# Splitting a norm's multiplications between GpSimd and VectorE: every other chunk instead of all of them

## The chip, the cores and the metric

The kernel runs on one core of one Trainium2 chip. Five engines work side by side, each on its own list of instructions in order: TensorE (PE in the rows; its weight loads are a row of their own, PEld), VectorE (DVE), ScalarE (ACT), GpSimd (POOL) and SyncE (SP, which here only issues DMAs). The metric is the device time of one execution in microseconds (us), the median of the runs.

## The reference, cut to what matters

Two transformer blocks follow each other on 256 tokens of width 1024 in float32. The second block has two layers; a layer is a SwiGLU feed-forward, a mixer (a convolution with latent attention in layer 0, sparse attention in layer 1) and a second feed-forward. In front of each of these stands a normalization with a modulation:

```python
def rms_norm_2(x, g):
    xf = x.astype(jnp.float32)
    y = xf * lax.rsqrt(jnp.mean(xf * xf, axis=-1, keepdims=True) + EPS)
    return (y * g.astype(jnp.float32)).astype(x.dtype)

def modulate(x, g, shift, scale):
    return rms_norm_2(x, g) * (1 + scale[:, None]) + shift[:, None]
...
        h = modulate(x, norm_g[l, 0], sh1, sc1)
        x = x + 0.5 * g1[:, None] * swiglu(h, ff_w13[l, 0], ff_w2[l, 0])
        h = modulate(x, norm_g[l, 1], sh2, sc2)
        ...
        x = x + g2[:, None] * y
        h = modulate(x, norm_g[l, 2], sh3, sc3)
        x = x + 0.5 * g3[:, None] * swiglu(h, ff_w13[l, 1], ff_w2[l, 1])
```

So per channel there is one gain (norm_g times 1 + scale) and one shift, and per token one factor, the reciprocal root of the mean square.

## The kernel before, in words

**Layout.** The residual stream `x` lies transposed in SBUF: the 1024 channels are 8 chunks of 128 partitions, the 256 tokens lie along the free dimension. The norm's output `h` is kept the same way, and split: a high part `hi` (rounded to the matmul's float32r) and a low part `lo`, the remainder. Each weight tile is split likewise into `whi` (ACT copies, line 359) and `wlo` (DVE subtracts, line 466), and a product is three matmuls or, in wide form, one of 512 columns and one of 256. Of weights, `pump` (line 453) splits three steps of 8 tiles ahead; the DVE half of a split is emitted one split later than the ACT half, so it never waits for it.

**The norm in two phases.** While the stage before ends, `norm_part` (line 627) takes each finished chunk c of x: `hi` and `lo` of x times gain go into `h` without the token factor (ACT at line 359, DVE at line 634), ACT squares the chunk, POOL adds the squares up (line 656). For the chunks in `st["keep"]` POOL also computes `xg` = x times gain into a buffer (line 640). The next stage's matmuls start on that `h` at once: the first two pairs of output tiles, the head, are computed without the token factor, and it is multiplied in when they are evacuated (`un`, line 532). Meanwhile `norm_sum` and `norm_bc` find the token factor and spread it over all partitions (`rbs`).

**`norm_apply`** (line 710) then makes the full `h` for the pairs that follow. For each chunk: the product `nt` = x times gain times `rbs`, either by POOL from `xg` and `rbs` (line 717) or, where no `xg` is there, by DVE in one fused instruction from x, the gain and `rbs` (line 719); then ACT writes `hi` = `nt` + shift (line 359), and DVE writes `lo` = `nt` + shift - `hi` (line 724, line 726 for the last chunk of a call). `lo` is emitted one chunk late.

**Order.** The program is one list of steps emitted in order, and each engine runs its own instructions in that order. `normed` (line 733) lays the steps out for a head of two pairs: three weight steps of the head, `norm_apply` on chunks 0 to 3, the head's fourth weight step (its emission puts one `whi` on ACT and one `wlo` on DVE), `norm_apply` on chunks 4 to 7, then `behind`: another split, and the evacuation of the head's second pair (line 531 and 532 on DVE, then ACT). Then come the pairs that read the full `h`, chunk by chunk from 0 to 7. Accumulators for them take turns in two PSUM buffers per tag; the fourth pair of a stage takes those that the second pair's evacuation frees.

**Five such norms** have a head of two pairs: in front of the mixer of layer 0 (near 620 us in the profile), the feed-forwards near 718, 910 and 1235 us, and the mixer of layer 1 (near 1102 us). The feed-forward near 428 us has a head of three pairs, and makes its `xg` in a step of its own (line 755); the norm at the end of the program keeps three chunks. In the feed-forwards a pair's evacuation also puts a fused step (line 1536) and a split of its result (line 392) on DVE.

Of the kernel before, what the change touches and what calls it, by code (L numbers as in the profile page):

```python
# [27 lines left out]
KD = D // P  # L28
# [275 lines left out]
class Kernel:  # L304
# [428 lines left out]
    def normed(self, st, gs, width=D, eps=1e-6, gain=None, shift=None, head=0, table=None, after=()):  # L733

        quiet = lambda xs: [setattr(x, "quiet", True) for x in xs]
        n1 = Step(lambda: self.norm_sum(st, width, eps, table=table))
        n2 = Step(lambda: self.norm_bc(st))
        if not head:
            quiet(gs[:2])
            return gs[:1] + [n1] + gs[1:2] + [n2] + gs[2:]  # L740

        def behind():
            self.pump(self.at, SPLIT_AHEAD + 1)
            st["behind"]()
            self.second()
        ap = [Step(lambda c=c: self.norm_apply(st, gain, lambda c: shift()[:, c:c + 1], c, c + 4)) for c in (0, 4)]
        e = 2 * head
        at = 2 if head == 2 else 3
        st["shift"] = shift
        if "two" not in st and head == 2:  # L750
            st["keep"] = range(KD)
        def times_gain():
            for c in range(KD):
                st["xg", c] = self.g("xg")
                self.nc.gpsimd.tensor_scalar(st["xg", c], self.x[:, c, :], gain(c), None, op0=OP.mult)
        out = gs[:1] + [n1] + ([Step(times_gain)] if head == 3 else []) + gs[1:at] + [n2] + gs[at:e - 1]
        out += [ap[0]] + gs[e - 1:e] + [ap[1], Step(behind)] + list(after) + gs[e:]
        quiet(gs[:e + 2])
        return out
# [1224 lines left out]
```

## Time and profile before

| | us |
|---|---|
| median of the runs shown | 1428.98 |
| lowest and highest of three runs | 1428.35, 1430.75 |
| the profiled execution, its own time | 1430.66 |
| its span, first to last instruction | 1428.9 |
| PE, DVE, ACT, POOL busy | 1400.3, 1139.2, 833.5, 213.4 |

The profile is one execution. "Busy" of PE says that a matmul was in flight; since matmuls are pipelined, a short wait can be hidden in it, and the weight loads (PEld) show it better. A row's "idle before" is the time in which an engine stood still ahead of the instruction, with the instruction that ended that. In a timeline, neighbouring instructions of one kind are merged: "x3" and the time from the start of the first to the end of the third.

### The profile page before, as it was taken

What the parts mean: (1) busy time and instruction counts of PE and PEld (TensorE: products, weight loads), DVE (VectorE), ACT (ScalarE), POOL (GpSimd) and SP (SyncE); (2) the same over time, 40 slices, a digit from 0 to 9 for tenths busy, and PEclk for the clock granted to TensorE, in tenths of its full rate; (3) what the DMA queues carried; (4) which work ended last, traced back from release to release, by engine and by line L of the source; (5) the groups of instructions that cost most, each with busy time, mean ns of one, the idle gap of its engine ahead of it and who ended that gap; (6) DMA issues with size and microseconds to landing.
All of it is one profiled execution on the core that took longest, in us unless ns stands there. A gap on an engine that the chain in (4) does not pass through costs nothing.

```text
span 1428.9 us, 23142 instructions
## 1 busy us (share of the span) xinstructions
PE 1400.3 (98%) x8998; PEld 1231.8 (86%) x8998; DVE 1139.2 (80%) x1911; ACT 833.5 (58%) x1605; POOL 213.4 (15%) x199
## 2 busy tenths in 40 slices
PE   8999999999999999999999999999999999999997
PEld 8887999888898888899888888888888877988886
DVE  7877877998879887878788888898887786887653
ACT  6646556765456665466675645665645565665542
POOL 3000101000142001421420003200033100500021
PEclk9999999999999999999999999999999999999999
DMA  9344534778775768744367778586776510376540
GB/s 330 123 148 147 207 129 167 270 268 319 296 290 193 293 263 307 267 160 150 117 236 265 270 284 305 202 314 254 277 289 227 207 60 31 148 266 235 199 181 34
DMA packets 46046, 311.66 MB, mean 218 GB/s; under 512 B 5232, under 2 KB 7024, under 8 KB 9072
## 3 DMA queue, kind: packets, MB, share of 16 engines
q1 hardware_dynamic: 45936, 310.19, 58.6%
q8 instruction: 70, 1.15, 0.3%
q14 instruction: 40, 0.33, 0.1%
HBM read 309.12 MB, written 1.05 MB: 217 GB/s over the span
## 4 chain that ended last, share of the span: by engine, by line
PE 83%; DVE 10%; ACT 3%; DMA 2%; issue 1%; POOL 0%; SPq 0%; POOLq 0%; ACTq 0%; DVEq 0%
PE mm L395 75%; DVE wlo L466 3%; PE o L395 2%; PE sc L395 2%; PE mmt L395 1%; DVE h L724 1%; DMA raw<-w_in 1%; PE ada L395 1%; DVE p L980 1%; PE pT L987 1%; PE ssum L395 1%; ACT p L359 1%; ACT whi L359 1%; DMA raw<-w 1%; DVE nm L969 1%
## 5 line engine op out<-in xcount | busy, mean ns | idle before, releaser
L395 PE MATMUL mm<-h,whi 128*128 128x512 f32 (+2 forms) x2400 | 708.3, 357 | 5.8 <-DVE h L724 3.8
L395 PE MATMUL mm<-h,wlo 128*128 128x256 f32 (+1 forms) x1960 | 553.1, 282 | 2.0 <-DVE wlo L466 2.0
L466 DVE TENSOR_TENSOR wlo<-raw,whi 128x1024 fp32r<-128x1024 f32 (+2 forms) x438 | 538.4, 1234 | 19.8 <-ACT whi L359 19.6
L359 ACT ACTIVATE whi<-raw 128x1024 fp32r<-128x1024 f32 (+2 forms) x438 | 452.8, 1046 | 138.6 <-DMA raw<-w 92.2
L395 PEld LDWEIGHTS mm<-h,whi 128*128 128x128 f32 x2400 | 424.7, 190 | 81.4 <-DVE h L724 7.4
L395 PEld LDWEIGHTS mm<-h,wlo 128*128 128x128 f32 x1960 | 372.4, 190 | 2.6 <-DVE wlo L466 2.6
L395 PE MATMUL mm<-gg,whi 128*128 128x512 f32 x960 | 340.1, 399 | 0.0
L395 PE MATMUL mm<-gg,wlo 128*128 128x256 f32 x960 | 269.6, 281 | 0.5 <-DVE wlo L466 0.5
L395 PEld LDWEIGHTS mm<-gg,whi 128*128 128x128 f32 x960 | 180.3, 188 | 48.2 <-ACT whi L359 1.7
L395 PEld LDWEIGHTS mm<-gg,wlo 128*128 128x128 f32 x960 | 181.3, 189 | 0.8 <-DVE wlo L466 0.8
L800 DVE SCALAR_TENSOR_TENSOR adacc<-raw,sc,adacc 128x1024 f32<-128x1024 f32 x126 | 165.5, 1314 | 0.4 <-ACT adacc L359 0.2
L640 POOL TENSOR_SCALAR xg<-x,M 128x256 f32<-128x256 f32 x40 | 63.0, 1575 | 557.8 <-DVE x L1407 557.8
L359 ACT ACTIVATE ft<-mm 128x256 f32<-128x256 f32 x190 | 67.5, 379 | 88.0 <-PE mm L395 87.9
L387 DVE TENSOR_TENSOR ft<-mm,ft 128x256 f32<-128x256 f32 x190 | 72.3, 419 | 44.4 <-ACT ft L359 44.4
L359 ACT ACTIVATE p<-sc,nm 128x128 f32<-128x128 f32 (+1 forms) x120 | 49.5, 423 | 58.4 <-DVE nm L969 24.6
L395 PE MATMUL mm<-o,whi 128*128 128x256 f32 x448 | 82.9, 286 | 0.1
L392 DVE TENSOR_TENSOR gg<-ft,gg 128x256 fp32r<-128x256 f32 x120 | 51.7, 442 | 34.1 <-ACT gg L359 34.0
L1407 DVE SCALAR_TENSOR_TENSOR x<-mm,M,x 128x256 f32<-128x256 f32 x80 | 38.5, 481 | 46.0 <-PE mm L395 44.8
L656 POOL TENSOR_TENSOR acc<-acc,sq 128x256 f32<-128x256 f32 x60 | 59.6, 997 | 94.8 <-ACT sq L359 71.2
L395 PEld LDWEIGHTS mm<-o,whi 128*128 128x128 f32 x448 | 70.1, 191 | 1.2 <-issue 0.3
L395 PE MATMUL mm<-o,wlo 128*128 128x256 f32 x224 | 63.3, 283 | 0.0
L359 ACT ACTIVATE gg<-ft 128x256 fp32r<-128x256 f32 x120 | 47.3, 407 | 26.5 <-DVE ft L1543 24.0
(278 smaller groups left out, 1459.9 us busy)
## 6 DMA issues: line engine op xcount, KB each, us to landing
raw<-w SPq DMA_DIRECT2D x132, 1024.0 KB, 4.9
raw<-ada SPq DMA_DIRECT2D x72, 1024.0 KB, 6.1
raw<-w_up SPq DMA_DIRECT2D x16, 1024.0 KB, 5.2
raw<-w_down SPq DMA_DIRECT2D x16, 1024.0 KB, 6.5
raw<-hy_in SPq DMA_DIRECT2D x8, 1024.0 KB, 5.2
raw<-w_in SPq DMA_DIRECT2D x6, 1024.0 KB, 8.9
raw<-nsa_in SPq DMA_DIRECT2D x6, 1024.0 KB, 6.9
raw<-w_ck SPq DMA_DIRECT2D x4, 1024.0 KB, 4.8
```

Source lines behind the costliest of these rows:

```text
L359: return self.nc.scalar.activation(out, in_, func, **k)
L387: self.nc.vector.tensor_add(t, ps[:, 1, :], t)
L392: self.nc.vector.tensor_tensor(lo, src, hi.bitcast(F), OP.subtract)
L395: self.nc.tensor.matmul(out, lhsT, rhs, start=start, stop=stop, skip_group_check=True)
L466: self.behind = lambda hi=hi[:, :b - a], lo=lo[:, :b - a], src=src: self.nc.vector.tensor_tensor(lo, src, hi.bitcast(F), OP.subtract)
L640: nc.gpsimd.tensor_scalar(st["xg", c], xc, gain(c), None, op0=OP.mult)
L656: nc.gpsimd.tensor_tensor(acc, st["acc" + key], sq, OP.add)
L724: nc.vector.scalar_tensor_tensor(*last, op0=OP.add, op1=OP.subtract)
L800: nc.vector.scalar_tensor_tensor(acc, src, scale, acc, op0=OP.mult, op1=OP.add)
L969: nc.vector.tensor_reduce(nm[:, tb, h:h + 1], part[tb], AX.X, OP.max, negate=True)
L980: nc.vector.tensor_tensor(p[tb], p[tb], r[:, tb, :, None].to_broadcast([P, 2, P + tb * P]), OP.mult)
L1407: nc.vector.scalar_tensor_tensor(xc, part, gate(m), xc, op0=OP.mult, op1=OP.add)
```

## The change

One line in `normed`. Where the set of chunks to keep was all eight, it becomes chunks 1, 3, 5 and 7, for the five norms with a head of two pairs:

```diff
         if "two" not in st and head == 2:
-            st["keep"] = range(KD)
+            st["keep"] = range(1, KD, 2)
```

In `norm_part`, POOL's `xg` of chunks 0, 2, 4 and 6 goes. In `norm_apply`, those chunks take the other branch, which was there already:

```python
            if ("xg", c) in st:
                nc.gpsimd.tensor_tensor(t, st.pop(("xg", c)), st["rbs"], OP.mult)
            else:
                nc.vector.scalar_tensor_tensor(t, self.x[:, c, :], gain(c), st["rbs"], op0=OP.mult, op1=OP.mult)
```

Per norm, four POOL multiplications by the gain and four by `rbs` go, and four fused DVE instructions come. The 256 columns of each, the ACT step and the `lo` step stay. Half as many `xg` buffers are taken from their ring.

## Rows read from the trace of the kernel before

**Rows 1.** Page: busy time of the engines; chain that ended last, by engine.

```profile
PE 1400.3 (98%) x8998; PEld 1231.8 (86%) x8998; DVE 1139.2 (80%) x1911; ACT 833.5 (58%) x1605; POOL 213.4 (15%) x199
...
PE 83%; DVE 10%; ACT 3%; DMA 2%; issue 1%; POOL 0%; SPq 0%; POOLq 0%; ACTq 0%; DVEq 0%
```

**Rows 2.** Waits of PEld and PE, 550 to 1250 us: total us, times, longest.

```profile
PEld mm L395 <- DVE h L724: 6.4, 14, 1.0
...
PE mm L395 <- DVE h L724: 3.0, 5, 0.8
...
PE mm L395 <- DVE wlo L466: 0.5, 1, 0.5
```

**Rows 3.** Tiles xg and nt: count, ns min/median/max, first and last start, shapes.

```profile
L640 POOL TENSOR_SCALAR xg<-x,M x40: 916/1089/2946, 555.0 to 1228.9; 128x256 f32<-128x256 f32 x40
...
L717 POOL TENSOR_TENSOR nt<-xg,rbs x48: 731/918/1818, 427.9 to 1241.9; 128x256 f32<-128x256 f32 x48
...
L724 DVE SCALAR_TENSOR_TENSOR h<-nt,M,h x36: 470/474/960, 436.3 to 1244.9; 128x256 fp32r<-128x256 f32 x36
...
L1610 DVE SCALAR_TENSOR_TENSOR nt<-un,colp,rbs x3: 480/481/485, 640.1 to 640.9; 128x256 f32<-128x256 f32 x3
```

**Rows 4.** Timeline of DVE, feed-forward norm near 1235: start, us, what.

```profile
1239.47 2.71 DVE L724 SCALAR_TENSOR_TENSOR h<-nt,M,h 128x256 fp32r<-128x256 f32 x3
...
1242.99 1.21 DVE L466 TENSOR_TENSOR wlo<-raw,whi 128x1024 fp32r<-128x1024 f32 x1
1244.12 1.26 DVE L724 SCALAR_TENSOR_TENSOR h<-nt,M,h 128x256 fp32r<-128x256 f32 x3
1245.31 0.47 DVE L726 SCALAR_TENSOR_TENSOR h<-nt,M,h 128x256 fp32r<-128x256 f32 x1
1245.71 1.21 DVE L466 TENSOR_TENSOR wlo<-raw,whi 128x1024 fp32r<-128x1024 f32 x1
...
1246.91 0.41 DVE L532 TENSOR_TENSOR un<-mm,rbs 128x256 f32<-128x256 f32 x1
```

**Rows 5.** Timeline of POOL and ACT, the same norm.

```profile
1235.27 7.51 POOL L717 TENSOR_TENSOR nt<-xg,rbs 128x256 f32<-128x256 f32 x8 [5.50 <-ACT rbs L359]
...
1239.30 0.51 ACT L359 ACTIVATE h<-nt,M 128x256 fp32r<-128x256 f32 x1 [0.65 <-POOL nt L717]
1239.72 1.04 ACT L359 ACTIVATE whi<-raw 128x1024 fp32r<-128x1024 f32 x1
```

**Rows 6.** Timeline of the weight loads, the same norm.

```profile
1240.48 0.19 PEld L395 LDWEIGHTS mm<-h,whi 128*128 128x128 f32 x1 [0.20 <-DVE h L724]
...
1244.65 0.19 PEld L395 LDWEIGHTS mm<-h,whi 128*128 128x128 f32 x1 [0.88 <-DVE h L724]
...
1247.46 0.19 PEld L395 LDWEIGHTS mm<-h,whi 128*128 128x128 f32 x1
```

**Rows 7.** Timeline of DVE and weight loads, norm of layer 0's mixer.

```profile
622.45 2.62 DVE L724 SCALAR_TENSOR_TENSOR h<-nt,M,h 128x256 fp32r<-128x256 f32 x3 [1.41 <-ACT h L359]
...
627.56 1.27 DVE L724 SCALAR_TENSOR_TENSOR h<-nt,M,h 128x256 fp32r<-128x256 f32 x3
...
628.09 0.19 PEld L395 LDWEIGHTS mm<-h,whi 128*128 128x128 f32 x1 [0.98 <-DVE h L724]
...
632.06 0.19 PEld L395 LDWEIGHTS ssum<-ones,sq 128*128 128x128 f32 x1 [0.27 <-ACT sq L359]
```

**Rows 8.** Timeline of DVE and weight loads, norm of layer 1's mixer.

```profile
1105.07 2.55 DVE L724 SCALAR_TENSOR_TENSOR h<-nt,M,h 128x256 fp32r<-128x256 f32 x3 [0.80 <-ACT h L359]
...
1111.11 0.19 PEld L395 LDWEIGHTS mm<-h,whi 128*128 128x128 f32 x1 [0.77 <-DVE h L724]
...
1117.63 0.47 PEld L395 LDWEIGHTS cm<-raw,bl 128*32 128x32 f32 x17 [0.42 <-issue]
```

**Rows 9.** Busy time by stretch: us, engines (x instructions), PEclk, DMA share, GB/s.

```profile
1124.00:1126.00 2.00, 0.52 (x4) 0.31 (x5) 0.62 (x3) 1.97 (x8) 0.00 (x0) 1.00 1.00 422
1126.00:1128.00 2.00, 2.00 (x14) 1.56 (x13) 0.58 (x3) 1.37 (x2) 0.00 (x0) 0.62 1.01 430
```

## The prediction

> **What bounds the kernel now.** I read the page first: PE is busy for 98% of the span, POOL for 15%, and the chain that ended last is PE for 83% and DVE for 10% [rows 1]. So work on POOL costs something only where PE waits for what POOL delays. The waits of the stretch that holds the five changed norms come next: the weight loads stood still for `h` of line 724 for 6.4 us in 14 places, PE itself for 3.0 us in 5, one place per norm [rows 2]. That is where the change acts, and about all that it could win there. Then I laid the timelines of one norm beside each other; the feed-forward norms near 718, 910 and 1235 us are alike (their waits agree within 0.05 us), so one stands for three.
>
> In that norm POOL makes its eight products from 1235.27 on, 7.51 us in all [rows 5]. DVE is busy with other steps until 1239.47; the fourth product is there by 1239.30, as ACT's step on it shows [rows 5]. The first four `lo` take some 0.9 us each, three in 2.71 [rows 4], although one takes 0.47 alone [rows 3]: they take turns with POOL's products. Behind them stands a `wlo` of 1.21, then the `lo` of chunks 4 to 7, in 0.40 steps, POOL having finished [rows 4]. PE waits 0.20 for chunk 0, a little for 1 to 3, and 0.88 for chunk 4, at 1244.65 [rows 6]. So the bound here is DVE's list of steps from 1239.47 to 1244.60, not POOL's products.
>
> **The change, part by part.** Gone: 20 of 40 `xg` on POOL and 20 of the 48 `nt` [rows 3]. Come: 20 fused `nt` on DVE. Their price is not in the trace for these operands; the nearest row, the same operation on the same shape with two inputs in SBUF, takes 0.48 (line 1610), and the upper bound is 0.96, what a fused step takes in turns with POOL [rows 3]. I take 0.48 and a step of 0.40 to the next, since in the feed-forwards POOL will have made its four products by 1239.3.
>
> The dearer part is order. A POOL product ran ahead of DVE's list; a DVE product stands in that list, just before ACT needs it: `nt` on DVE, `hi` on ACT (0.51, [rows 5]), `lo` on DVE. Each such turn costs 0.48 + 0.50 and two hand-overs of 0.05 at most (a `lo` ends at 1244.60, the load behind it starts at 1244.65, [rows 4, 6]) before the `lo` can start, and only an older `lo` fills part of it. ACT also stands: its `hi` of the odd chunks and a `whi` are queued behind a `hi` that waits for DVE. That `whi` moves from 1239.72 to about 1242.3 [rows 5]; the `wlo` made from it comes only after chunk 7's `lo`, so nobody waits.
>
> *Feed-forward norm, with hand-overs of 0.05.* First call: `nt`0 1239.47, `hi`0 1240.00, `lo`0 1240.55, `nt`2 1240.95, `lo`1 1241.35, `hi`2 1241.48, `lo`2 1242.03, `lo`3 1242.43 to 1242.90. Without POOL in the way the four `lo` end at 1242.9 instead of about 1243.07, a gain of 0.2. Then `wlo` to 1244.04. Second call: `nt`4 1243.96, `hi`4 1244.49, `lo`4 1245.04 to 1245.51, against 1244.60 now, so PE takes up chunk 4 0.9 later. `nt`6 1245.44, `lo`5, then `hi`6 1245.97, `lo`6 1246.52, `lo`7 to 1247.39, against 1245.78 [rows 4]. From there DVE is 1.6 late: `wlo`, then the evacuation of the head's second pair, which ended at 1247.32 and would end at 1248.93. That frees the PSUM buffer which the fourth pair needs; PE began it at 1247.46 [rows 4, 6], 0.14 behind the release, and would now begin at about 1249.0: 1.5 late. With hand-overs of 0.03 it is 1.4. I take 1.4; three norms give +4.2. Ends for one norm: +0.8, if only chunk 4 counts and the evacuation does not, and +1.9, if one `nt` on the path costs 0.96.
>
> *Mixer norms.* Here DVE stands idle before its first `lo`, 1.41 and 0.80 us, for ACT [rows 7, 8]; `nt`0 fits into that hole and the first turn is nearly free. In layer 0, `lo`0 stays at 622.45 and still takes turns with POOL, to 623.3; then, with the durations above, `nt`2 623.2, `hi`2 623.7, `lo`2 624.3, `lo`3 624.7, `wlo` 625.1, `nt`4 626.2, `hi`4 626.7, `lo`4 627.2 to 627.7. Chunk 4 comes to PE at 627.75 instead of 628.09, but `nt`6, `hi`6 and `lo`6 put the end of `lo`7 at 629.5, where three steps of 0.40 and a last 0.47 from 627.56 give 629.2 now. Behind it wait the `un`, the square and the sum at which PE already stands, 632.06 [rows 7]: net +0.3. In layer 1 the same walk starts worse, as the hole is shorter and POOL is still busy in it: `hi`0 and `lo`0 move 0.6 back, to 1105.7, chunk 4 stays near 1111.1 (0.1 earlier), `lo`7 is 0.5 late, and through `un` and the block copies this reaches the matmuls at 1117.63, at which PE already waits [rows 8]: +0.5. Ends: -0.3 to +0.5 and -0.1 to +0.8.
>
> *The `xg` that go.* Twenty fewer POOL instructions ahead of the norms spare DVE turns of up to 0.5 each. Who would gain is a PE that waits for `wlo` or for the first `h`: in the whole stretch it waits for `wlo` once, 0.5 us [rows 2]. Splits run three steps ahead, so I put this at nothing; the ends are -0.5 and 0. If that cover were gone, 20 times 0.5 on DVE would be the most to win. Fewer buffers in the ring can only release waits; nothing in the rows waits there.
>
> Sum: 4.2 + 0.3 + 0.5 = +5.0 us; ends 2.4 - 0.4 - 0.5 = +1.5 and 5.7 + 1.3 = +7.0. The profiled execution took 1430.66, so it would become 1435.7; the median of the runs, 1.7 lower, becomes 1434.0. About 0.2%, 2.9 us, is what a measurement can tell from no change.
>
> **The rivals.** *Half the price (+2.1, 1431.1):* the fourth pair does not wait for the evacuation, or DVE makes its delay good before; then each feed-forward norm costs 0.8, the mixer of layer 0 gives 0.3 back and that of layer 1 nothing. For it: the evacuation misses PE by a hair now. Against it: that hair is 0.14, and the delay of 1.6 has no idle DVE time in it to vanish into. This is within what can be told.
>
> *The turns with POOL are the price (-1.7, 1427.3):* four `lo` per norm fall from 0.95 to 0.47, 1.9 us, four `nt` of 0.40 come, 1.6: -0.3 per norm and a little more in the mixers, if the ACT turns were hidden. The Trainium skill speaks for this ("SBUF — State Buffer", Who interferes with whom): a DVE instruction with two SBUF inputs and a GpSimd one that reads SBUF exclude each other, and the loser waits for the whole instruction. The trace agrees: 0.47 alone, 0.96 in turns [rows 3]. But the rule prices the turn, not the order. Against the rival: in the second call there is no POOL left to get rid of, three `lo` take 1.26 now [rows 4], and that call is where `nt`4 and its turn fall.
>
> *The other side, faster (about -4.5, 1424.5):* the waits at line 724 vanish, between the 3.0 of PE and the 6.4 of the loads [rows 2]. The place is chunk 4 of the feed-forwards; it decides if `lo`4 ends before PE comes there, some 1243.1 (1240.28, where its wait for chunk 0 began, and four chunks of 0.70, a quarter of the time from 1244.65 to 1247.46 [rows 6]). The `wlo` ahead of `lo`4 ends at 1244.20 now [rows 4], later than that, so DVE would have to reach 1239.47 a good microsecond earlier, by fewer turns with POOL; but the four products that remain fall into just that stretch.
>
> *The clock (1435.7 and more):* after 2 us in which PE was busy for 0.52, the granted clock fell to 0.62 in 1126 to 1128, that is, part of it at 1.2 instead of 2.4 GHz [rows 9]. The wait at chunk 4 would be about 1.5 us, with PE busy ahead of it. One such fall, some 3 us at half speed, costs about 1.7.
>
> *The change does nothing:* the set is read when the steps run, after all norms are laid out, as the 40 `xg` show [rows 3]; I give it no more than 0.01.
>
> **How the numbers follow.** Forecast 0.62; half the price 0.16; turns 0.09; waits vanish 0.05; clock 0.07; nothing 0.01. The time is the forecast's, 1434.0. A range from 1430.0 to 1437.0 holds the forecast, the half price and the first clock fall and leaves out the turns, the vanished waits and more falls, under 0.2. Faster by over 0.2%: the vanished waits and a little of the turns, 0.06. Within: half the price, the rest of the turns, nothing: 0.24. Slower: forecast and clock, 0.70.
>
> **What would show it.** Twenty `xg` (of M) and 28 `nt` on POOL, 20 `nt` on DVE at line 719 of about 0.48; `lo` at line 724 almost all at 0.47; new waits of ACT's `h` for DVE's `nt`, and DVE's waits at line 724 for ACT up from two to a dozen or more; the weight loads' wait at chunk 4 of the feed-forwards up from 0.88 to about 1.5, with a new wait at the fourth pair for line 532. If chunk 4 waits no longer than before, the working is wrong; if it waits longer and the time stays, something later absorbs it.

## The result, and the profile after

| | us |
|---|---|
| changed kernel, median of 5 runs | 1437.29 (1435.77 to 1439.21) |
| kernel before, median of 5 runs beside it | 1430.75 (1428.35 to 1431.55) |
| ratio, 95% interval | 1.0054 (1.0043 to 1.0064) |
| profiled execution after, its own time and span | 1438.58, 1436.8 |

Slower, by 7.7 us (6.2 to 9.2) as the ratio has it; the two medians of the table lie 6.5 apart, and the traces below find 7.1 at the five norms. The ratio, which comes with an interval, is used from here on. The forecast was slower by 5.0 us and a time of 1434.0. The direction was right; the time lies 0.3 us above the range. The 3.3 us between 1434.0 and 1437.29 are by the ratio 2.7 for the price of the change and 0.6 for the base (it puts the kernel before at 1429.6 in these runs, I started from 1428.98); by the medians they are 1.5 and 1.8.

The page of the changed kernel: busy time of the engines, then the chain that ended last, by engine, as in [rows 1].

```profile
PE 1402.5 (98%) x8998; PEld 1232.2 (86%) x8998; DVE 1138.5 (79%) x1931; ACT 833.3 (58%) x1605; POOL 160.3 (11%) x159
...
PE 80%; DVE 12%; ACT 3%; DMA 2%; issue 2%; POOL 0%; SPq 0%; POOLq 0%; ACTq 0%; DVEq 0%
```

DVE has 20 instructions more and is busy for 0.7 us less; POOL lost 53 us of busy time, and the kernel did not get faster by it. DVE's share of the chain rose from 10% to 12%. Where a busier DVE isn't the reason, its waits must be. Tiles of the norms, then the waits between 550 and 1260 us by engine (total us, times, longest), as in [rows 2, 3]; the last line is of the kernel before.

```profile
L640 POOL TENSOR_SCALAR xg<-x,M x20: 916/1006/2938, 564.2 to 1234.9; 128x256 f32<-128x256 f32 x20
L717 POOL TENSOR_TENSOR nt<-xg,rbs x28: 734/918/1818, 428.8 to 1243.6; 128x256 f32<-128x256 f32 x28
L719 DVE SCALAR_TENSOR_TENSOR nt<-x,M,rbs x20: 472/479/967, 621.6 to 1251.7; 128x256 f32<-128x256 f32 x20
L724 DVE SCALAR_TENSOR_TENSOR h<-nt,M,h x36: 474/485/960, 437.2 to 1252.8; 128x256 fp32r<-128x256 f32 x36
...
ACT h L359 <- DVE nt L719: 20.7, 18, 2.6
DVE h L724 <- ACT h L359: 8.8, 19, 0.9
PEld mm L395 <- DVE h L724: 8.6, 10, 1.7
PE mm L395 <- DVE h L724: 6.1, 6, 1.4
PE mm L395 <- DVE un L532: 1.1, 3, 0.4
...
DVE h L724 <- ACT h L359: 2.2, 2, 1.4
```

ACT now waits for DVE's `nt` in 18 places, and DVE for ACT's `hi` in 19 places where it was 2 (2.2 us). PE's own wait for `h` doubled, from 3.0 to 6.1 us, and three waits for line 532 are new.

The feed-forward norm near 1241 us, DVE's timeline (start, us, what; in brackets the idle time before it and what ended it). It answers to [rows 4]; the first two lines are of the kernel before and stand where its list begins.

```profile
1235.22 0.42 DVE L532 TENSOR_TENSOR un<-mm,rbs 128x256 f32<-128x256 f32 x1 [1.05 <-ACT rbs L359]
1236.28 0.71 DVE L1536 SCALAR_TENSOR_TENSOR ft<-un,unb,ft 128x256 f32<-128x256 f32 x1 [0.23 <-ACT ft L359]
...
1241.30 0.42 DVE L532 TENSOR_TENSOR un<-mm,rbs 128x256 f32<-128x256 f32 x1 [1.05 <-ACT rbs L359]
1242.36 0.72 DVE L1536 SCALAR_TENSOR_TENSOR ft<-un,unb,ft 128x256 f32<-128x256 f32 x1 [0.23 <-ACT ft L359]
...
1245.56 0.47 DVE L719 SCALAR_TENSOR_TENSOR nt<-x,M,rbs 128x256 f32<-128x256 f32 x1
1246.67 0.48 DVE L724 SCALAR_TENSOR_TENSOR h<-nt,M,h 128x256 fp32r<-128x256 f32 x1 [0.64 <-ACT h L359]
1247.07 0.48 DVE L719 SCALAR_TENSOR_TENSOR nt<-x,M,rbs 128x256 f32<-128x256 f32 x1
1247.47 0.48 DVE L724 SCALAR_TENSOR_TENSOR h<-nt,M,h 128x256 fp32r<-128x256 f32 x1
1248.21 0.48 DVE L724 SCALAR_TENSOR_TENSOR h<-nt,M,h 128x256 fp32r<-128x256 f32 x1 [0.26 <-ACT h L359]
1248.61 0.49 DVE L726 SCALAR_TENSOR_TENSOR h<-nt,M,h 128x256 fp32r<-128x256 f32 x1
1249.01 1.22 DVE L466 TENSOR_TENSOR wlo<-raw,whi 128x1024 fp32r<-128x1024 f32 x1
1250.15 0.48 DVE L719 SCALAR_TENSOR_TENSOR nt<-x,M,rbs 128x256 f32<-128x256 f32 x1
1251.27 0.48 DVE L724 SCALAR_TENSOR_TENSOR h<-nt,M,h 128x256 fp32r<-128x256 f32 x1 [0.64 <-ACT h L359]
1251.67 0.48 DVE L719 SCALAR_TENSOR_TENSOR nt<-x,M,rbs 128x256 f32<-128x256 f32 x1
...
1252.79 0.48 DVE L724 SCALAR_TENSOR_TENSOR h<-nt,M,h 128x256 fp32r<-128x256 f32 x1 [0.24 <-ACT h L359]
1253.19 0.48 DVE L726 SCALAR_TENSOR_TENSOR h<-nt,M,h 128x256 fp32r<-128x256 f32 x1
1253.59 1.22 DVE L466 TENSOR_TENSOR wlo<-raw,whi 128x1024 fp32r<-128x1024 f32 x1
...
1254.80 0.41 DVE L532 TENSOR_TENSOR un<-mm,rbs 128x256 f32<-128x256 f32 x1
```

Each call of `norm_apply` holds DVE idle twice, 0.64 behind its first `nt` and some 0.25 in front of its third `lo`. From the start of the first pair's first `un` to the end of the second pair's first `un` the list takes 1255.21 - 1241.30 = 13.91 us; before it took 12.10. DVE stood idle in it for 0.23 us before, and for 2.01 now; the rest, in which it was busy, is 11.87 and 11.90. So four products were added per norm and the busy time stayed, and 1.78 of the 1.81 us are DVE standing for ACT. That is the balance over both calls. The first call, from its first step to the end of the `wlo` behind it, takes as long as before (4.73 us then, 4.67 now): turns with POOL that go pay there for two products and two waits. The delay arises in the second call, where no turn was left to go: 1.66 us then, 3.52 now, of which 0.88 are waits for ACT and some 0.8 are two products. The weight loads of the same norm show where that comes out, with [rows 6]:

```profile
1247.21 0.19 PEld L395 LDWEIGHTS mm<-h,whi 128*128 128x128 f32 x1 [0.85 <-DVE h L724]
...
1251.81 0.19 PEld L395 LDWEIGHTS mm<-h,whi 128*128 128x128 f32 x1 [1.72 <-DVE h L724]
...
1255.33 0.19 PEld L395 LDWEIGHTS mm<-h,whi 128*128 128x128 f32 x1 [0.65 <-PE mm L395]
1255.36 0.47 PE L395 MATMUL mm<-h,whi 128*128 128x512 f32 x1 [0.36 <-DVE un L532]
```

Counted from the first `un`, chunk 0 reaches PE 0.65 later than before (5.91 against 5.26), chunk 4 1.08 later, and the fourth pair 1.79 later (14.03 against 12.24). The wait of its weight load is named after PE, and PE's matmul row names `un` of line 532. I read this as PE standing until the second pair's evacuation frees the PSUM buffers; an experiment below tests it.

### The profile page after: what moved, and what is told of

Its sections match the earlier page's. It is cut to its first block, busy times and chain, and to the rows that moved or that the text cites. A ratio compares the mean times of both kernels' runs of the same rounds, so it can differ in the third digit from the quotient of the medians.

```text
span 1436.8 us, 23113 instructions
## 1 busy us (share of the span) xinstructions
PE 1402.5 (98%) x8998; PEld 1232.2 (86%) x8998; DVE 1138.5 (79%) x1931; ACT 833.3 (58%) x1605; POOL 160.3 (11%) x159
## 4 chain that ended last, share of the span: by engine, by line
PE 80%; DVE 12%; ACT 3%; DMA 2%; issue 2%; POOL 0%; SPq 0%; POOLq 0%; ACTq 0%; DVEq 0%
PE mm L395 72%; DVE wlo L466 4%; PE o L395 2%; PE mmt L395 1%; PE sc L395 1%; DMA raw<-w 1%; DVE h L724 1%; PE ada L395 1%; ACT h L359 1%; DVE p L980 1%; ACT p L359 1%; PE ssum L395 1%; DVE adacc L800 1%; ACT whi L359 1%; DVE nm L969 1%
## 5 line engine op out<-in xcount | busy, mean ns | idle before, releaser
L466 DVE TENSOR_TENSOR wlo<-raw,whi 128x1024 fp32r<-128x1024 f32 (+2 forms) x438 | 539.0, 1235 | 22.1 <-ACT whi L359 21.8
L640 POOL TENSOR_SCALAR xg<-x,M 128x256 f32<-128x256 f32 x20 | 30.6, 1529 | 446.6 <-DVE x L1407 446.6
L359 ACT ACTIVATE ft<-ft 128x256 f32<-128x256 f32 x111 | 44.5, 413 | 31.6 <-DVE ft L1485 26.7
```

Source lines behind the costliest of these rows:

```text
L359: return self.nc.scalar.activation(out, in_, func, **k)
L466: self.behind = lambda hi=hi[:, :b - a], lo=lo[:, :b - a], src=src: self.nc.vector.tensor_tensor(lo, src, hi.bitcast(F), OP.subtract)
L640: nc.gpsimd.tensor_scalar(st["xg", c], xc, gain(c), None, op0=OP.mult)
```

## The experiments

The theory (order): a DVE product puts a trip DVE, ACT, DVE into DVE's own list, and the list stands idle for it. The main rival (DVE time): 20 products at 0.40 are 8.0 us, and they simply lengthen the list. The total of 7.7 fits the rival better than it fitted my forecast, so the total can't decide. A second question was which of PE's waits carries the price. All times are medians beside the kernel before on the same chip.

**The same products, in another place** (e_hoist in later expectations). All of DVE's products of a norm are emitted at the start of its first call:

```diff
+        if c0 == 0:
+            for c in range(KD):
+                if ("xg", c) not in st:
+                    t = st["nt", c] = self.g("nt")
+                    nc.vector.scalar_tensor_tensor(t, self.x[:, c, :], gain(c), st["rbs"], op0=OP.mult, op1=OP.mult)
...
-                nc.vector.scalar_tensor_tensor(t, self.x[:, c, :], gain(c), st["rbs"], op0=OP.mult, op1=OP.mult)
+                t = st.pop(("nt", c))
```

> The changed kernel with one thing moved: the four fused DVE products of a norm (chunks 0, 2, 4, 6) are all issued at the start of the first call, ahead of the first lo, instead of each just before ACT needs it. Same instructions, same number, POOL as in the changed kernel. Theory order (the cost is the DVE-ACT-DVE turn inside DVE's list, above all at chunk 4): by the walk, lo of chunk 4 ends some 0.3 us earlier than in the kernel before and the last lo 0.3 earlier, so each feed-forward norm gives 0.2 to 0.3, the mixer norms 0.6 to 1.0 each, as their wait at chunk 4 goes: about -2 against the kernel before (1428 to 1429), and 8 to 9 us under the changed kernel. Rival DVE time (20 more instructions of 0.40 on the engine that sets the end, 8 us, wherever they stand): no change against the changed kernel, +6 to +8 against before.

Measured: 1426.43 against 1429.52, ratio 0.9982 (0.9973 to 0.9991). DVE near 1237 us, and the weight loads' only wait in that norm (the products are line 718 here, their `lo` line 729):

```profile
1237.25 1.66 DVE L718 SCALAR_TENSOR_TENSOR nt<-x,M,rbs 128x256 f32<-128x256 f32 x4
1238.83 1.26 DVE L729 SCALAR_TENSOR_TENSOR h<-nt,M,h 128x256 fp32r<-128x256 f32 x3
...
1240.42 1.21 DVE L466 TENSOR_TENSOR wlo<-raw,whi 128x1024 fp32r<-128x1024 f32 x1
1241.55 1.27 DVE L729 SCALAR_TENSOR_TENSOR h<-nt,M,h 128x256 fp32r<-128x256 f32 x3
...
1244.34 0.41 DVE L532 TENSOR_TENSOR un<-mm,rbs 128x256 f32<-128x256 f32 x1
...
1239.36 0.19 PEld L395 LDWEIGHTS mm<-h,whi 128*128 128x128 f32 x1 [1.31 <-DVE h L729]
```

The same 20 products, now slightly faster than the kernel before: no idle time behind them, `lo` in 0.40 steps, chunk 4 without a wait. The rival of DVE time, +6 to +8 wherever the products stand, falls; the order holds. The products take their buffers from the ring of the `xg` here; no wait for a buffer shows in the rows of DVE or POOL. Chunk 0 pays instead (1.31), as four products stand ahead of its `lo`.

**More products on DVE.** All eight on DVE, in their old places:

```diff
-            st["keep"] = range(1, KD, 2)
+            st["keep"] = ()
```

> All eight products of each of the five norms on DVE, none on POOL (no xg, no POOL nt). Theory order: with neighbouring chunks on DVE the next product fills the wait for ACT, and DVE has no POOL to take turns with, so it reaches the norm's steps 1.3 us earlier; chunk 4 near the kernel before (0.4 earlier), last lo 0.2 to 0.5 later: 0 to +0.5 per norm, 0 to +2 in all, that is 5 us under the changed kernel although it does twice as much on DVE. Rival DVE time: 40 more DVE instructions instead of 20, so twice the changed kernel's cost, +13 to +16 against before.

Measured: 1438.51 against 1429.52, ratio 1.0065 (1.0051 to 1.0079). Neither expectation. DVE:

```profile
1250.30 0.88 DVE L719 SCALAR_TENSOR_TENSOR nt<-x,M,rbs 128x256 f32<-128x256 f32 x2
1251.41 0.48 DVE L724 SCALAR_TENSOR_TENSOR h<-nt,M,h 128x256 fp32r<-128x256 f32 x1 [0.24 <-ACT h L359]
1251.82 0.48 DVE L719 SCALAR_TENSOR_TENSOR nt<-x,M,rbs 128x256 f32<-128x256 f32 x1
...
1253.75 0.49 DVE L726 SCALAR_TENSOR_TENSOR h<-nt,M,h 128x256 fp32r<-128x256 f32 x1 [0.26 <-ACT h L359]
```

The second product fills a part of the first trip (0.64 falls to 0.24), where I had let it fill all. With POOL out of the way DVE comes to its first product 2.93 behind the first `un` instead of 4.26. But in the second call, where POOL was out of the way before, too, nothing pays for the products: from `nt`4 to the end of the last `lo` it takes 3.94 us, 3.52 in the changed kernel and 1.66 before. Of the 2.28 more, four products are 1.6 and two waits for ACT 0.50. So the rival has a part of the truth here: DVE time counts where no turn with POOL is given back for it.

**Other chunks.** In the first kernel POOL keeps the even chunks, so the first product of each call comes ready; in the second it keeps the whole second call:

```diff
-            st["keep"] = range(1, KD, 2)
+            st["keep"] = range(0, KD, 2)
...
-            st["keep"] = range(1, KD, 2)
+            st["keep"] = range(4, KD)
```

> The mirror image of the change: chunks 0, 2, 4, 6 stay on POOL and 1, 3, 5, 7 go to DVE. As many instructions on each engine as in the changed kernel; but the first chunk of each call is a POOL product that is ready, so the lo of chunk 4 needs no turn. Theory order: chunk 4 comes as in the kernel before (0.1 earlier), the last lo 0.9 later because of the products and the turn of chunk 7, so the wait at chunk 4 stays and the one at the fourth pair comes: +0.8 to +1.0 per feed-forward norm, +0.5 per mixer norm, +3 to +4 in all. Rival DVE time: as the changed kernel, +6 to +8.

> Again half and half, but chunks 0 to 3 on DVE and 4 to 7 on POOL. Theory order: in the first call neighbouring DVE products fill each other's wait for ACT, in the second call POOL's products have long been ready and no turn is left: chunk 4 0.3 later than before in the feed-forwards, 0.5 to 0.8 earlier in the mixers, whose hole in DVE takes the first two products: +0.3 per feed-forward norm, -0.6 per mixer norm, -1 to +1 in all (no change to be told). Rival DVE time: as the changed kernel, +6 to +8.

Measured: even chunks 1434.28, ratio 1.0033 (1.0021 to 1.0046); the upper four 1430.34, ratio 1.0007 (0.9998 to 1.0017), both against 1429.52. Four products per norm on DVE cost 7.7, 4.7 and 1.0 us by the chunks they are of, and -2.6 moved to the front: it goes by where they stand, not by how many they are. With the upper four on POOL chunk 4 waits as before:

```profile
1239.76 0.19 PEld L395 LDWEIGHTS mm<-h,whi 128*128 128x128 f32 x1 [0.91 <-DVE h L724]
...
1243.62 0.19 PEld L395 LDWEIGHTS mm<-h,whi 128*128 128x128 f32 x1 [0.87 <-DVE h L724]
```

**One kind of norm at a time.** The new set in the feed-forwards alone, as shown, then in the mixers alone, with the two sets exchanged:

```diff
-            st["keep"] = range(1, KD, 2)
+            st["keep"] = range(1, KD, 2) if len(gs) > 40 else range(KD)
```

> The change in the three feed-forward norms (near 718, 910, 1235 us) alone; the two mixer norms keep all eight products on POOL. From the two traces, the delay of the weight loads grows by 1.76, 1.81 and 1.84 us at these norms: +5 to +6 against the kernel before. Rival, that the difference lies elsewhere (start of the program, where the two profiles differ by 0.9; clock falls; DVE turns in the stages ahead of the norms): a sum of the two parts that isn't the whole, and this one under +4.

> The change in the two mixer norms (near 620 and 1102 us) alone. From the traces +0.75 and +1.0: +1.5 to +2 against the kernel before, if no clock fall comes or goes (one is worth 1.7). The prediction had +0.8 for both.

Measured: feed-forwards 1435.86, ratio 1.0039 (1.0025 to 1.0052); mixers 1431.81, ratio 1.0011 (1.0003 to 1.002), both against 1430.53. That is 5.6 and 1.6 us, 7.2 together: within the intervals the parts add up to the whole, 7.7.

**Which wait carries it.** The fourth pair takes its PSUM buffers from other tags, so that it doesn't depend on the second pair's evacuation:

```diff
-                            state["ps"] = [self.ps("mm", [P, 2, S], "mm"), self.ps("mm", [P, 2, S], "T")]
+                            tg = ("S", "O") if head == 2 and pr == 3 else ("mm", "T")
+                            state["ps"] = [self.ps("mm", [P, 2, S], n) for n in tg]
```

> The changed kernel, but in the feed-forwards with a head of two pairs the fourth pair accumulates in two other PSUM buffers (tags S and O) than those which the late evacuation of the head's second pair frees. If the second wait (0.65 us at the fourth pair in each of the three) is for that evacuation, it goes: 1.5 to 2 us under the changed kernel, about +5 against before, and no wait over 0.2 us of the weight loads there. Rival, that the fourth pair waits for its weights' low part (the split is as late as the evacuation) or that the delay is only passed on to the next late step: the same time as the changed kernel.

Measured: 1434.62 against 1430.53, ratio 1.0032 (1.002 to 1.0045). Its weight loads, chunk 0, chunk 4 and the fourth pair (line numbers one higher):

```profile
1243.28 0.19 PEld L395 LDWEIGHTS mm<-h,whi 128*128 128x128 f32 x1 [0.85 <-DVE h L725]
...
1247.88 0.19 PEld L395 LDWEIGHTS mm<-h,whi 128*128 128x128 f32 x1 [1.71 <-DVE h L725]
...
1250.79 0.19 PEld L395 LDWEIGHTS mm<-h,whi 128*128 128x128 f32 x1
```

The wait at the fourth pair is gone, the two for `h` are as in the changed kernel, and the fourth pair begins 1.18 us later than in the kernel before instead of 1.79. So the wait was for the evacuation, and a third of a feed-forward norm's price passes through it and two thirds through `h` itself.

**Towards something better.** In the feed-forwards a split of the first pair's result (line 392) stands ahead of the products. Three kernels hold it back until behind the norm: on top of the products at the front (e_hoist_gg in the expectations); with the kernel before's set (all eight on POOL); and as the first of these, with chunk 6's product moved behind the first `lo`.

```diff
-                self.deferred.append(lambda: self.split(g[0], g[1], s))
+                late = self.late if pr == 0 and head == 2 else self.deferred
+                late.append(lambda: self.split(g[0], g[1], s))
...
+            self.deferred, self.late = self.late + self.deferred, []
```

> The kernel with the four products issued first (e_hoist), and in the three feed-forward norms the split of the first pair's result (ACT copy, DVE subtract in turns with POOL 0.95 us; needed only in the down projection) is held back until behind the norm. If DVE's list up to the lo of chunk 4 sets the end there, it starts 0.4 to 0.9 us earlier and each feed-forward norm gives that: 1.2 to 2.7 us under e_hoist, -4 to -5 against before. If the start of the head's end (PE still at the head) sets it, no change against e_hoist.

> The kernel before (all eight products on POOL), with only the split of the first pair's result held back until behind the norm in the three feed-forward norms. DVE comes to its first lo some 0.9 us earlier, but meets more of POOL's products there: the first four lo and the wlo behind them still take turns, and lo of chunk 4 comes about 0.4 earlier: -1 to -1.5 against before. If it gives as much as e_hoist_gg (-4), the moved products count for nothing there and the held-back split is all of it; if nothing, the split was covered.

> e_hoist_gg with the product of chunk 6 issued behind the first lo instead of ahead of it, so that the lo of chunk 0, for which PE waits 0.9 us in each feed-forward norm there, comes 0.4 earlier; the lo of chunk 4 stays. If chunk 0 sets the end of these norms, 0.2 to 0.4 per norm: -5 against before. If chunk 4 then waits instead, no change against e_hoist_gg, -4.

Measured: 1426.06 against 1430.53, ratio 0.9972 (0.9962 to 0.9982); 1429.09 against 1429.82, ratio 0.9993 (0.9983 to 1.0002); 1425.9 against 1429.82, ratio 0.9974 (0.9965 to 0.9983). Holding the split back alone can't be told from nothing. Together with the products at the front it takes 0.28% off the kernel before, which is more than the held-back split alone gives; against the products at the front alone (0.18%) the intervals overlap. Moving chunk 6's product shortens the wait for chunk 0 from 0.92 to 0.53, but chunk 4 then waits 0.27, and the time stays.

**The ledger.** For each kernel: DVE's list in the third feed-forward norm (as above), its idle time, and PE's way from the last weight load of the head to the first of the fourth pair. Then what these traces predict for the whole: three times the difference of PE's way, and for the mixers the differences of the ways from the sum of squares ahead of the layer-0 norm to that behind it, and from the first `un` of the layer-1 norm to the block matmuls (0.73 and 0.97 in the changed kernel). The last column is what the ratio says. The kernels stand in the order in which they were told.

| kernel | list, us | idle in it | PE's way | traces say | measured (interval) |
|---|---|---|---|---|---|
| before | 12.10 | 0.23 | 7.37 | | |
| changed | 13.91 | 2.01 | 9.16 | +7.1 | +7.7 (6.2 to 9.2) |
| products at the front | 11.76 | 0.24 | 7.11 | -2.2 | -2.6 (-3.9 to -1.3) |
| all on DVE | 13.39 | 1.25 | 8.63 | +5.9 | +9.3 (7.3 to 11.3) |
| even on POOL | 13.11 | 1.25 | 8.36 | +3.7 | +4.7 (3.0 to 6.6) |
| upper on POOL | 12.51 | 0.75 | 7.75 | +0.3 | +1.0 (-0.3 to 2.4) |
| feed-forwards only | 13.91 | 2.01 | 9.16 | +5.3 | +5.6 (3.6 to 7.4) |
| mixers only | 12.11 | 0.24 | 7.37 | +1.7 | +1.6 (0.4 to 2.9) |
| other PSUM buffers | 13.90 | 2.01 | 8.55 | +5.2 | +4.6 (2.9 to 6.4) |
| front, split held back | 11.37 | 0.24 | 6.72 | -3.4 | -4.0 (-5.4 to -2.6) |
| before, split held back | 11.78 | 0.24 | 7.03 | -1.0 | -1.0 (-2.4 to 0.3) |
| front, chunk 6 later | 11.37 | 0.24 | 6.62 | -3.7 | -3.7 (-5.0 to -2.4) |

List less idle is 11.5 to 12.1 us in the rows down to the other PSUM buffers: adding four products, or eight, hardly changes how long DVE works in this list, since the turns with POOL that go pay for them. (Below, the split and its turn with POOL have left the list.) What differs most is the idle time. One row doesn't close: with all on DVE 3.4 us are missing. Behind the mixer norms its profile shows two stretches at half the granted clock where the kernel before shows one, and one such stretch costs some 1.5 (last section). Over the whole execution each of the two profiles has three, though, so this is no answer for the total, and the 3.4 stay open.

The traces' column counts the norms alone. Laid beside each other from start to end, the profiles of the changed kernel and of the kernel before differ by 7.9 us: 7.1 at the five norms, 0.9 in the first 60 us, where the edit does nothing, and smaller shifts that cancel.

## Why the prediction was right in kind and short in size

**What held.** The mechanism: a trip DVE, ACT, DVE in DVE's own list, felt by PE at chunk 4 and at the fourth pair. The signs all came: 20 `xg`, 28 `nt` on POOL, 20 `nt` at line 719 of 0.48, the `lo` back at 0.48, ACT's waits for DVE, DVE's 19 waits for ACT, chunk 4 of the feed-forwards at 1.72 where I put about 1.5, and the fourth pair's wait for line 532. The walk through a feed-forward norm started right: from first `un` to first step 4.25 before and 4.26 after. The rule of the Trainium skill on shared reads ("SBUF — State Buffer", Who interferes with whom) named the gain correctly, and this trace agrees: of the 36 steps of line 724, 14 took over 0.9 us before and 2 do now, and DVE's busy time in the list stayed at 11.9 with four products more. As the prediction said, it prices the turns with POOL and not the order.

**What failed: the size of the turn DVE, ACT, DVE.** It is the term of +4.2, three times 1.4, and the mixers' +0.3 and +0.5 with it. Delays of the weight loads behind each norm against those ahead of it, the two traces laid beside each other (the expectation for the feed-forwards alone has them from other loads, up to 0.03 apart):

| norm | taken | measured |
|---|---|---|
| mixer, layer 0 | +0.3 | +0.73 |
| feed-forwards near 718, 910, 1235 | +1.4 each | +1.79, +1.79, +1.82 |
| mixer, layer 1 | +0.5 | +0.97 |
| sum | +5.0 | +7.1 |

In the feed-forwards 0.4 is missing per norm, and most of it can be found step by step in the norm near 1245. "Two hand-overs of 0.05 at most" was the first error: I read it from a `lo` and the weight load behind it, another pair of engines. From DVE to ACT it is twice that. ACT's timeline:

```profile
1246.13 0.91 ACT L359 ACTIVATE h<-nt,M 128x256 fp32r<-128x256 f32 x2 [2.60 <-DVE nt L719]
1247.67 0.91 ACT L359 ACTIVATE h<-nt,M 128x256 fp32r<-128x256 f32 x2 [0.63 <-DVE nt L719]
...
1250.72 0.91 ACT L359 ACTIVATE h<-nt,M 128x256 fp32r<-128x256 f32 x2 [1.20 <-DVE nt L719]
1252.24 0.91 ACT L359 ACTIVATE h<-nt,M 128x256 fp32r<-128x256 f32 x2 [0.61 <-DVE nt L719]
```

The first `nt` ends at 1245.56 + 0.47 = 1246.03 and `hi` starts at 1246.13; the second ends at 1247.55, `hi` starts at 1247.67. All four are on the path. From ACT back to DVE it is 0.03, which gives 0.02 of each 0.05 back; with that and some hundredths in the steps the walk came out 0.2 short over four turns: its `lo`7 ended 7.92 behind the first step, the trace says 8.11. Next, I let the fourth pair start 0.07 behind the evacuation; it starts 0.12 behind it, nearly as before (0.14): what I took for slack was hand-over. And I took 1.4 where the walk with 0.05 gave 1.5, on a hand-over of 0.03 that is right only from ACT back to DVE. 0.2, 0.05 and 0.1 make most of the 0.4.

**The mixers.** The 0.96 that I kept as an upper bound for a product did come there (0.96 and 0.97 for the first one, in turns with POOL), in DVE's hole as put. In layer 0 the walk was right up to `nt`4 (7.08 behind the first `un`, walk 7.12); then ACT starts late, and all later steps carry it:

```profile
626.82 0.47 DVE L719 SCALAR_TENSOR_TENSOR nt<-x,M,rbs 128x256 f32<-128x256 f32 x1
628.21 0.48 DVE L724 SCALAR_TENSOR_TENSOR h<-nt,M,h 128x256 fp32r<-128x256 f32 x1 [0.91 <-ACT h L359]
...
627.67 0.91 ACT L359 ACTIVATE h<-nt,M 128x256 fp32r<-128x256 f32 x2 [1.62 <-DVE nt L719]
...
633.45 0.52 PEld L395 LDWEIGHTS ssum<-ones,sq 128*128 128x128 f32 x4 [0.92 <-ACT sq L359]
```

`nt` is there at 627.29, `hi` starts at 627.67: 0.38, where 0.10 is the hand-over elsewhere. The same gap, 0.37 or 0.38, stands in all four profiles in which DVE makes chunk 4's product just before ACT needs it; what holds ACT there isn't settled. In layer 1 the same points came 0.1 (first `lo`), 0.3 (`lo`4) and 0.5 us (`lo`7) later than put, again growing turn by turn.

**The small terms.** The `xg` that go, taken at nothing: the traces don't separate them. Ahead of the layer-0 norm this profile gained 0.3 on the kernel before, and the others lie between a gain of 0.8 and a loss of 0.4, the largest gain with all `xg` in place. "Fewer buffers in the ring can only release waits" was wrong in one place: POOL's last product in layer 0 waited 0.67 for a DVE `lo`, as I read it for the buffer which that `lo` frees; ACT took the product only 4.9 us after it was there, so PE didn't feel it. The clock, priced as a rival for the longer wait at chunk 4: behind those waits of 1.70 to 1.72 the granted clock stayed at 1.00. A stretch at half speed came near 635 instead and the one near 1126 [rows 9] went, +1.5 and -1.5 in the delays, so in this profile the two cancel.

**The rivals.** Half the price: the evacuation does count, for a third. The turns with POOL: that gain is real and about as large as the products' cost, but the trips weren't hidden. Once the products stood at the front they were, and the kernel came out 2.6 us faster, near that rival's -1.7. The other side, faster: the waits for `h` did not vanish but grew from 3.0 to 6.1 of PE's time.

## What to carry to other kernels

Before moving a step onto the engine that also makes the next but one, write that engine's list with its waits: a step whose result goes out to another engine and comes back costs the round trip wherever no older work fills it. Here the list's idle time was the price, because the turns with POOL that went paid for the steps that came; where none went, as in the second call, the steps' own time came on top. Where the moved steps are independent, issue them together ahead of the first round trip; here that alone turned +0.54% into -0.18%. Take each hand-over from rows of the same two engines in the same direction, and multiply by the turns on the path.

## What was not expected of the hardware

Hand-overs differ by direction: DVE to ACT 0.10 and 0.12 us in the rows above, ACT to DVE 0.03 (the first of the two `hi` in its row takes 0.51: 1246.13 + 0.51 = 1246.64, `lo` 1246.67).

The granted clock fell behind a stretch in which PE was busy for more than half of the time and never waited longer than 0.92. Changed kernel (us; busy us of PE, PEld, DVE, ACT, POOL with instructions; granted clock; DMA share; GB/s):

```profile
632.00:634.00 2.00, 1.16 (x11) 1.08 (x10) 1.68 (x4) 1.81 (x5) 0.00 (x0) 1.00 0.00 0
635.00:638.00 3.00, 3.00 (x16) 3.00 (x16) 2.01 (x5) 2.97 (x5) 0.00 (x0) 0.50 0.42 161
1134.00:1137.00 3.00, 3.00 (x28) 2.84 (x25) 2.04 (x7) 1.40 (x5) 0.00 (x0) 1.00 1.03 431
```

At 635 PE is full and at 1.2 instead of 2.4 GHz; near 1134, where the same work follows the stretch of [rows 9], it stays at 2.4. The same place doesn't always do the same. In the kernel with other PSUM buffers the weight loads stood 0.91 in the place where they stood 0.92 here, and the granted clock behind it, 633 to 638, was 1.00. With the products at the front and in the feed-forwards alone neither place shows such a stretch, with all products on DVE one shows near 634 and one near 1133. Near 131 us, ahead of every edit, eight of the twelve profiles show one (0.50 from 130 to 132 in the kernel before) and four do not (1.00 in the kernel with the upper four on POOL, which gains 1.6 us on the kernel before at that place). Some 1.5 us of difference between two profiles can come from one such fall.
